# Operands of each stage prepared in the stage ahead of it, in a one-core transformer block on Trainium2

## Chip, cores, metric

One core of a Trainium2 chip runs the whole program. The metric is the device time of one execution in microseconds, as the median of several runs. Engines are named as in the profile: PE is TensorE (PEld its weight loads), DVE is VectorE, ACT is ScalarE, POOL is GpSimd, SP is SyncE, which here only issues loads and stores.

## The reference

One layer on x of 1024 tokens x 1024 features, float32. Retention runs over 4 heads in chunks of 128 tokens.

```python
h = rmsnorm(x, ln_mix)
z = h @ w_in                       # q | k | v | g | pu | gate_logits
ret_n = group_norm(retention_chunkwise(rotary(q), rotary(k), v)) * gn_gain
y_ret  = (silu(g) * ret_n) @ w_ret_up
y_pool = multiscale_pool(pu, pool_w, pool_scale) @ w_pool_up
gates  = sigmoid(gate_logits + b_gate)
x = x + (gates[..., :D] * y_ret + gates[..., D:] * y_pool) @ w_o
h2 = rmsnorm(x, ln_mlp)
x = x + square(relu(h2 @ w_up)) @ w_down        # w_up 1024 x 4096, w_down 4096 x 1024
return rmsnorm(x, ln_final)
```

## The kernel before

Features lie on the 128 partitions, tokens along the row, and most tiles are 128 x 512: one block of features by one half of the tokens. Every operand of a matmul is kept as a pair of a rounded high part and the remainder: `split_pair` (L131 to L133) has ACT write the copy (L132) and DVE the difference (L133); `split_weights` (L88 to L93) does so for 128 x 1024 weights. A product takes three matmuls for each contraction tile (`PASSES`): high by high, high by remainder, remainder by high.

The stages follow one another: q, k, v and retention; the swish gates (`ps_g`), with the pooling and `mixed_blocks` (block sums `hx` of the input for the gates) in the same loop over f; the branch gates, `gates(i)` for i < 8; the pool projection (`ps_yp`); the retention projection (`ps_yr`); the output projection (`ps_o`), which also makes the row sums of squares; up, `up(j)` for j < 16; down, in four sweeps over the same 16 j; the final norm.

Branch gates and up use `seven` (L178 to L219), which computes a 2 x 2 block product with seven block products instead of eight. It loads the weights `raw`, makes four sums of their blocks on DVE (`sum`, L204 to L215), splits each operand right ahead of its product, and collects in four PSUM banks `ps_X`, `ps_Y`, `ps_Z`, `ps_V`; each product is 12 matmuls (L191). `done` takes a finished bank over: for up a squared relu, scaled by the row's root R, and block sums of it (`act`), which POOL's queue stores to DRAM. The rest `u_up`, `tmp_up` are differences of finished banks.

Down uses the same seven products, written out by hand (L793 to L875), with `step` (L781) as one product into four banks, over four sweeps: X and Y, X and Z, V and Z, V. For each j it loads rows of `w_down` (`wa_`, `wb_`, `wc_`, `wd_`) and the stored blocks (`ad`), makes the weight sums (`sa`, `sb`, `sc`) and splits all (`da`, `db`, `ds`, `dt`), just ahead of that j's matmuls. After the second and third sweep the banks are added to the residual `x1b`, reloaded from DRAM, and ACT squares it (`add_squares`, L634 to L638). The last four j of the fourth sweep are taken for one output tile after the other (L875 to L887).

`token_rstd` makes the reciprocal root mean square of the tokens: PE transposes the sums (L160, four 128 x 128), DVE reduces them over 512 columns (L164) and scales (L142), POOL takes the power -1/2 (L145), PE spreads the result over the partitions (L151). `finish` (L732 to L747) multiplies by the gain on ACT (L738) and by the root on DVE or POOL (L743) and stores (L744).

A scheduler sets the order on each engine, when the program is built, from its own model of the times; on the chip every engine, and SP's queue of loads, then works through its list in order, and a row that waits holds up the rows behind it. Tiles come from pools with a fixed number of buffers (`h` and `r` 16 each, weights 4, `raw` 2, PSUM 5 banks and 3 more), so a load can start when the buffer's old tile has been read.

Of the kernel before, what the change touches and what calls it, by code (L numbers as in the profile page):

```python
# [38 lines left out]
def block_kernel(ctx: ExitStack, tc: tile.TileContext, a: dict, out: bass.AP):  # L39
# [19 lines left out]
    make_identity(nc, ident)  # L59
    nhalf = consts.tile([P, 4], F32, name="nhalf")  # L60
# [80 lines left out]
    def rstd_of(ssq, name, n):  # L141
        nc.vector.tensor_scalar(ssq, ssq, 1.0 / D, EPS, ALU.mult, ALU.add)  # L142
        tag = f"rstd_{name}" if name[0] == "a" else "rstd"
        rstd = stat.tile([P, n], F32, tag=tag, name=f"rstd_{name}")
        nc.gpsimd.tensor_tensor(rstd, ssq, nhalf[:, :n], ALU.pow)  # L145
        return rstd
# [9 lines left out]
    def token_rstd(sums, name):  # L156
        n = sums.shape[1] // P
# [6 lines left out]
        nc.vector.tensor_reduce(  # L164
            ssq, ps[:, : n * P].rearrange("p (t k) -> p t k", k=P),
            mybir.AxisListType.X, ALU.add,
        )
        return spread(rstd_of(ssq, name, n), n, name)
# [9 lines left out]
    def seven(name, src, moving, done):  # L178
# [5 lines left out]
        s1, s2, s3, s4 = (sums[:, i, :] for i in range(4))  # L184

        def mult(ps, src, x, start=True):
            w = pair_tile("a", f"w{x}_{name}")
            split_pair(w, src)
            for k in range(4):
                for n, (sa, sb) in enumerate(PASSES):  # L190
                    nc.tensor.matmul(  # L191
                        ps, w[:, sa, k * P : (k + 1) * P], moving[x][k][:, sb, :],
# [9 lines left out]
        mult(X, a11, B11)  # L202
        nc.scalar.activation(p1, X, AF.Copy)
        nc.vector.tensor_tensor(s1, a21, a22, ALU.add)  # L204
        nc.vector.tensor_tensor(s2, s1, a11, ALU.add)
        mult(Y, s2, T2)
        nc.vector.tensor_tensor(u2, p1, Y, ALU.subtract)
        mult(X, a12, B21, start=False)
        done(0, 0, X)
        mult(Z, s1, T1)  # L210
        nc.vector.tensor_tensor(u4, u2, Z, ALU.add)
        nc.vector.tensor_tensor(s3, a11, a21, ALU.add)
        mult(V, s3, T3)
        done(1, 1, V, u4)
        nc.vector.tensor_tensor(s4, a12, s2, ALU.add)  # L215
        mult(Z, s4, B22, start=False)
        done(0, 1, Z, u2)
        mult(V, a22, T4, start=False)
# [316 lines left out]
    for f in range(KT):  # L535
# [5 lines left out]
        if f in (2, 4, 5, 6):  # L541
            mixed_blocks((2, 4, 5, 6).index(f))
# [4 lines left out]
    def gates(i):  # L547
# [21 lines left out]
        seven(f"sg{i}", a["w_gate"][i], hx, done)  # L569
# [5 lines left out]
    ypT = []  # L575
    for f in range(4):
        y = a_tile("a", f"ypf{f}")
        nc.sync.dma_start(y, yp_dram[f])
        ypT.append([])
        for half in range(2):  # L580
            dst = pair_tile("h", f"ypT{f}_{half}")
            split_pair(dst, y[:, half * HALF : (half + 1) * HALF])
            ypT[f].append(dst)
# [103 lines left out]
    for half in range(2):  # L687
        sl = slice(half * HALF, (half + 1) * HALF)
        nc.vector.tensor_copy(R2[:, sl], token_rstd(sums2[:, half, :], f"b{half}"))


    def up(j):
# [24 lines left out]
        seven(f"up{j}", a["w_up"][j], h2, done)  # L717

    for j in range(NJ):
        up(j)  # L720


    outT = out.rearrange("(f p) t -> f p t", p=P)
    x1 = [None] * KT
# [7 lines left out]
    def finish(t0, n, R3, sizes):  # L732
        f0 = 0
        for size in sizes:
            o = a_tile("r", f"o_{t0}_{f0}", shape=(P, size, n))
            for i in range(size):
                f = f0 + i
                nc.scalar.activation(  # L738
                    o[:, i, :], x1[f][:, t0 : t0 + n], AF.Copy,
                    scale=vec[:, V_LNF + f : V_LNF + f + 1],  # L740
                )
# [77 lines left out]
    for i in UNITS:  # L819
        load_x1(i)  # L820
# [161 lines left out]
```

## Time and profile before

| | |
|---|---|
| Median of 3 runs | 1407.29 us (1406.32 to 1408.37) |
| Profiled execution | 1409.86 us |
| Its span, first to last instruction | 1408.1 us |
| Mean granted clock of PE | 0.988 |
| PE, DVE, ACT, POOL busy | 97%, 69%, 39%, 6% |
| Chain that ended last | PE 91%, DVE 4%, issue 2% |

Busy time is the time in which an instruction of the engine runs, matmuls at half clock included. The granted clock is TensorE's clock as a share of the full one. A wait is put down to the instruction that released it.

### The profile page before, as it was taken

The page shows a single profiled execution, that of the slowest core. Times are in us where ns is not written, and L with a number is a line of the kernel's source. Part 1 is how long each engine was busy: PE and PEld are TensorE (multiplying, and loading weights), DVE is VectorE, ACT ScalarE, POOL GpSimd, SP SyncE. Part 2 cuts the span into 40 slices and gives each one's busy share as a digit, 9 for nine tenths or more (in the row PEclk, how much of TensorE's full clock was granted, in tenths as well). Part 3 has the DMA queues.
Part 4 walks back from the last instruction along what each step waited for, and adds up shares of the span by engine and source line. Part 5 has one row for each costly group of instructions (what it writes and reads, how often), then busy time and mean ns, then how long its engine had stood idle before and what let it go on. Part 6 is the DMA issues. An engine that isn't in the chain of part 4 may idle for free.

```text
span 1408.1 us, 17330 instructions
## 1 busy us (share of the span) xinstructions
PE 1369.3 (97%) x6560; PEld 1147.6 (81%) x6560; DVE 969.9 (69%) x1605; ACT 545.5 (39%) x912; POOL 83.4 (6%) x139
## 2 busy tenths in 40 slices
PE   9999999999899999999999999999998999999985
PEld 6998999888688887888887788888887888878874
DVE  5766667767867645654558777877777867669583
ACT  6232424332534333321435333333333544335272
POOL 0000000100000000000000111111010000000001
PEclk9999999999999999999999999999999999999998
DMA  9111011232522328533322344343469977739251
GB/s 352 47 60 58 33 31 31 98 120 75 179 104 95 117 105 310 183 124 131 105 90 90 113 164 165 139 160 132 146 243 393 390 249 244 259 129 366 89 179 60
DMA packets 63572, 216.68 MB, mean 154 GB/s; under 512 B 7232, under 2 KB 9280, under 8 KB 59904
## 3 DMA queue, kind: packets, MB, share of 16 engines
q1 hardware_dynamic: 47648, 158.66, 32.2%
q0 software_dynamic: 15696, 56.89, 10.6%
q8 instruction: 51, 0.84, 0.3%
q14 instruction: 33, 0.27, 0.1%
q10 hardware_dynamic: 144, 0.03, 0.0%
HBM read 163.12 MB, written 52.43 MB: 153 GB/s over the span
## 4 chain that ended last, share of the span: by engine, by line
PE 91%; DVE 4%; issue 2%; DMA 1%; ACT 1%; POOL 0%; POOLq 0%; DVEq 0%; SPq 0%; ACTq 0%
PE ps_v L119 7%; PE ps_o L119 6%; PE ps_yr L119 6%; PE ps_dnX L781 6%; PE ps_Zup L191 6%; PE ps_Vup L191 6%; PE ps_Xup L191 6%; PE ps_dnV L781 6%; PE ps_dnZ L781 5%; PE ps_g L119 4%; PE ps_qT L119 3%; PE ps_Yup L191 3%; PE ps_pu L119 3%; PE ps_kT L119 3%; PE ps_dnY L781 3%; PE ps_Xsg L191 3%
## 5 line engine op out<-in xcount | busy, mean ns | idle before, releaser
L781 PE MATMUL ps_dnX<-db,da 128*128 128x512 f32 x384 | 94.1, 394 | 4.3 <-ACT db L132 4.3
L119 PE MATMUL ps_v<-w_v_hi,hT 128*128 128x256 f32 x512 | 95.9, 284 | 0.0
L191 PE MATMUL ps_Xup<-mv,w_up 128*128 128x512 f32 x384 | 94.3, 390 | 1.7 <-DVE w_up L133 1.5
L191 PE MATMUL ps_Zup<-mv,w_up 128*128 128x512 f32 x384 | 93.1, 390 | 0.3 <-ACT w_up L132 0.3
L191 PE MATMUL ps_Vup<-mv,w_up 128*128 128x512 f32 x384 | 93.0, 389 | 0.0
L119 PE MATMUL ps_g<-hT,w_g 128*128 128x512 f32 x384 | 90.6, 391 | 0.0
L781 PEld LDWEIGHTS ps_dnX<-db,da 128*128 128x128 f32 x384 | 73.1, 191 | 20.1 <-ACT db L132 4.7
L119 PE MATMUL ps_o<-mixT,w_o 128*128 128x512 f32 x384 | 87.5, 389 | 0.0
L119 PE MATMUL ps_yr<-retT,w_ret 128*128 128x512 f32 x384 | 87.2, 389 | 0.0
L191 PEld LDWEIGHTS ps_Xup<-mv,w_up 128*128 128x128 f32 x384 | 71.8, 188 | 17.3 <-DVE w_up L133 2.0
L191 PEld LDWEIGHTS ps_Zup<-mv,w_up 128*128 128x128 f32 x384 | 71.9, 188 | 15.9 <-ACT w_up L132 1.1
L119 PEld LDWEIGHTS ps_yr<-retT,w_ret 128*128 128x128 f32 x384 | 72.1, 188 | 15.0
L191 PEld LDWEIGHTS ps_Vup<-mv,w_up 128*128 128x128 f32 x384 | 72.1, 188 | 14.9
L119 PEld LDWEIGHTS ps_o<-mixT,w_o 128*128 128x128 f32 x384 | 72.0, 188 | 14.9
L119 PEld LDWEIGHTS ps_g<-hT,w_g 128*128 128x128 f32 x384 | 71.4, 188 | 14.4
L119 PEld LDWEIGHTS ps_v<-w_v_hi,hT 128*128 128x128 f32 x512 | 80.8, 192 | 0.0
L119 PE MATMUL ps_v<-w_v_lo,hT 128*128 128x256 f32 x256 | 72.7, 284 | 0.0
L699 ACT ACTIVATE act<-act 128x512 f32<-128x512 f32 x64 | 40.4, 632 | 76.9 <-DVE act L698 76.5
L132 ACT ACTIVATE w_up<-sum_up 128x512 fp32r<-128x512 f32 x64 | 39.8, 629 | 60.6 <-PE ps_Zup L191 23.6
L119 PE MATMUL ps_qT<-hT,w_qT 128*128 128x512 f32 x192 | 49.9, 407 | 1.8 <-ACT hT L136 1.5
L781 PE MATMUL ps_dnV<-dt,da 128*128 128x512 f32 (+1 forms) x204 | 46.3, 388 | 4.9 <-ACT dt L132 4.4
L132 ACT ACTIVATE w_up<-raw_up 128x512 fp32r<-128x512 f32 x48 | 30.1, 630 | 52.5 <-PE ps_Zup L191 25.5
(254 smaller groups left out, 2825.8 us busy)
## 6 DMA issues: line engine op xcount, KB each, us to landing
act_dram<-act POOLq DMA_DIRECT2D x48, 512.0 KB, 3.3
ad<-act_dram SPq DMA_DIRECT2D x48, 512.0 KB, 5.8
raw_up<-in_w_up_dram SPq DMA_DIRECT2D x16, 1024.0 KB, 5.0
raw_sg<-in_w_gate_dram SPq DMA_DIRECT2D x8, 1024.0 KB, 4.9
sg_dram<-sg POOLq DMA_DIRECT2D x16, 512.0 KB, 2.9
wa_lo<-in_w_down_dram SPq DMA_DIRECT2D x16, 512.0 KB, 9.0
wb_hi<-in_w_down_dram SPq DMA_DIRECT2D x16, 512.0 KB, 4.2
wc_lo<-in_w_down_dram SPq DMA_DIRECT2D x16, 512.0 KB, 5.2
```

The lines of the kernel that those rows point to most:

```text
L119: nc.tensor.matmul(ps, stationary(k, sa), moving(k, sb), start=i == 0, stop=i == n - 1)
L132: nc.scalar.activation(dst[:, 0, :], src, AF.Copy)
L191: nc.tensor.matmul(ps, w[:, sa, k * P : (k + 1) * P], moving[x][k][:, sb, :], start=start and k == 0 and n == 0, stop=k == 3 and n == 2, s ...
L699: nc.scalar.activation(dst, dst, AF.Square)
L781: nc.tensor.matmul(banks[i][:, c0 : c0 + n], w[:, sa, i * P : (i + 1) * P], x[:, sb, c0 : c0 + n], start=start and j == 0 and m == 0, stop ...
```

## The change

Six things change.

1. `token_rstd`: instead of the transposes and the reduce, matmuls with a column of ones write the sums of each 128 tokens into one PSUM column, which DVE scales straight from PSUM; with two parts, both are accumulated.
2. `seven` can take the last contraction tile of its first four products last (`late`, for gates(0) and up(0)), and has a hook `after`, called once X is done.
3. `mixed_blocks` runs at f = 1 to 4 instead of 2, 4, 5, 6.
4. The pooled operands are loaded and split in the last gate unit (`load_pooled`), the first two steps of down in the last unit of up (`begin_down`).
5. Down's operands are made from one list over all sweeps, three steps ahead (`prepare`); residual additions and squares are spread over the sweeps' steps.
6. At the end, the gains are applied ahead, DVE alone multiplies by the root, two tiles to an instruction and straight from PSUM, and the square of the last tile goes into the row sums as a second matmul.

```diff
@@ token_rstd @@
-            nc.tensor.transpose(
-                ps[:, t * P : (t + 1) * P], sums[:, t * P : (t + 1) * P], ident
-            )
-        ssq = stat.tile([P, n], F32, tag="ssq", name=f"ssq_{name}")
-        nc.vector.tensor_reduce(
...
+            for i, part in enumerate(sums):
+                nc.tensor.matmul(
+                    ps[:, t : t + 1], part[:, t * P : (t + 1) * P], ones[:, :1],
+                    start=i == 0, stop=i == len(sums) - 1,
+                )
+        return spread(rstd_of(ps[:, :n], name, n), n, name)
@@ seven @@
+        groups = {
+            B11: (X, (a11,)),
+            T2: (Y, (s2, (s1, a21, a22), (s2, s1, a11))),
+            T1: (Z, (s1,)),
+            T3: (V, (s3, (s3, a11, a21))),
+        }
+        rest = range(4)
+        if late:
+            rest = (3,)
+            for x, (ps, made) in groups.items():
+                stationary(x, *made)
+                mult(ps, x, range(3))
...
         done(0, 0, X)
-        mult(Z, s1, T1)
+        if after:
+            after()
+        opening(T1)
@@ swish loop @@
-        if f in (2, 4, 5, 6):
-            mixed_blocks((2, 4, 5, 6).index(f))
+        if 1 <= f <= 4:
+            mixed_blocks(f - 1)
@@ gates, up @@
+            f"sg{i}", a["w_gate"][i], hx, done, late=i == 0,
+            after=load_pooled if i == KT - 1 else None,
...
+            f"up{j}", a["w_up"][j], h2, done, late=j == 0,
+            after=begin_down if j == NJ - 1 else None,
@@ down @@
+    plan = [(ops, j) for ops in (operands_a, operands_b, operands_c, operands_d) for j in range(NJ)]
+    ready = []
+
+    def prepare(n):
+        while len(ready) < min(n, len(plan)):
+            ops, j = plan[len(ready)]
+            ready.append(ops(j))
+
+    def begin_down():
+        prepare(2)
...
+    def run(n, j, first, second=None, start=(True, True)):
+        prepare(n + 3)
+        for banks, wx, st in zip((first, second), ready[n], start):
+            step(banks, wx, j, start=st)
...
+    def residual(j):
+        if j % 2 == 0 and j < 8:
+            load_x1(j // 2)
+        if j % 2 == 1 and 2 < j < 11:
+            i = j // 2 - 1
+            add(x1[i][:, TH], x1[i][:, TH], u2[i])
...
+    def second_residual(j):
+        if j < 4:
+            add_squares(sums_all[:, T0], x1[j][:, T0], j == 0, f"z0_{j}", spare)
@@ end @@
+    def finish(i, t0, n, R3):
+        o = gained[t0 >= HALF, i][:, :, t0 % HALF : t0 % HALF + n]
+        nc.vector.tensor_tensor(
+            o, o, R3.rearrange("p (o t) -> p o t", o=1).to_broadcast([P, 2, n]), ALU.mult
+        )
...
+    for c0 in (0, 256):
+        c = slice(c0, c0 + 256)
+        last(3, c0, 256)
+        sq = spare(f"sq_z0_7_{c0}")[:, :256]
+        nc.scalar.activation(sq, x1[7][:, c], AF.Square)
...
+        ps = token_rstd([sums_all[:, c], sq], f"z0_{c0}")
+        pieces.append((c0, ps))
+    for c0, ps in pieces:
+        for i in UNITS:
+            finish(i, c0, 256, ps)
```

Where the instructions go. On PE at the change from up to down, before (`ps_Vup` collects the last of the seven products of up(15), with its weights `w_up`; `ps_dnX` are down's first banks):

```order
2326 L191 MATMUL ps_Zup_8270<-mv_3_6052,w_up_8359 128x512 x3
2327 L191 MATMUL ps_Vup_8271<-mv_0_5574,w_up_8382 128x512 x3
2328 L191 MATMUL ps_Vup_8271<-mv_1_5737,w_up_8382 128x512 x3
2329 L191 MATMUL ps_Vup_8271<-mv_2_5900,w_up_8382 128x512 x3
2330 L191 MATMUL ps_Vup_8271<-mv_3_6063,w_up_8382 128x512 x3
2331 L781 MATMUL ps_dnX_8403<-db_0_8422,da_0_8419 128x512
2332 L781 MATMUL ps_dnX_8404<-db_0_8422,da_0_8419 128x512
2333 L781 MATMUL ps_dnX_8405<-db_0_8422,da_0_8419 128x512
2334 L781 MATMUL ps_dnX_8406<-db_0_8422,da_0_8419 128x512
```

and now:

```order
2319 L195 MATMUL ps_Vup_8269<-mv_1_5725,w_up_8379 128x512 x3
2320 L195 MATMUL ps_Vup_8269<-mv_2_5888,w_up_8379 128x512 x3
2321 L195 MATMUL ps_Vup_8269<-mv_3_6051,w_up_8379 128x512 x3
2322 L854 MATMUL ps_dnX_8443<-db_0_8331,da_0_8328 128x512
2323 L854 MATMUL ps_dnX_8444<-db_0_8331,da_0_8328 128x512
2324 L854 MATMUL ps_dnX_8445<-db_0_8331,da_0_8328 128x512
2325 L854 MATMUL ps_dnX_8443<-db_0_8331,da_0_8328 128x512 x2
2326 L854 MATMUL ps_dnX_8444<-db_0_8331,da_0_8328 128x512 x2
2327 L854 MATMUL ps_dnX_8445<-db_0_8331,da_0_8328 128x512 x2
```

The first step of down now follows the fifth of the seven products; behind two steps into three banks each come the last two products of up(15), `ps_Zup` and `ps_Vup`, and then the fourth banks of those steps.

On ACT at the same place, before (`act_15` are the squares of the last unit of up, `da` to `dt` the copies for down):

```order
615 L699 ACTIVATE act_14_8116<-act_14_8116 128x512
616 L699 ACTIVATE act_15_8259<-act_15_8259 128x512
617 L699 ACTIVATE act_15_8261<-act_15_8261 128x512 x2
618 L699 ACTIVATE act_15_8260<-act_15_8260 128x512
619 L132 ACTIVATE da_0_8419<-wa_lo_8411 128x512
620 L132 ACTIVATE db_0_8422<-ad_0_8416 128x512
621 L132 ACTIVATE ds_0_8439<-sa_8418 128x512
```

and now:

```order
614 L730 ACTIVATE act_15_8257<-act_15_8257 128x512
615 L134 ACTIVATE da_0_8328<-wa_lo_8321 128x512
616 L134 ACTIVATE db_0_8331<-ad_0_8326 128x512
617 L134 ACTIVATE ds_0_8337<-sa_8334 128x512
618 L134 ACTIVATE dt_0_8340<-ad_0_8326 128x512
619 L134 ACTIVATE da_1_8347<-wa_lo_8343 128x512
620 L134 ACTIVATE db_1_8350<-ad_1_8345 128x512
621 L134 ACTIVATE ds_1_8356<-sa_8353 128x512
622 L134 ACTIVATE dt_1_8359<-ad_1_8345 128x512
623 L730 ACTIVATE act_15_8259<-act_15_8259 128x512 x2
624 L730 ACTIVATE act_15_8258<-act_15_8258 128x512
625 L134 ACTIVATE da_2_8458<-wa_lo_8451 128x512
```

The eight copies for the first two steps stand ahead of the last three squares; those of the third step are behind them.

On ACT at the change from the third to the fourth sweep, before (`sums_` and `sq_z` are squares of the residual, `o` its multiplication by the gain):

```order
820 L637 ACTIVATE sq_z_5_10614<-x1b_9840 128x512
821 L637 ACTIVATE sq_z_6_10619<-x1b_9843 128x512
822 L637 ACTIVATE sq_z_7_10624<-x1b_9846 128x512
823 L637 ACTIVATE sq_z_0_10629<-x1b_9837 128x512
824 L738 ACTIVATE o_0_10751<-x1b_9837,vec 128x512
825 L637 ACTIVATE sq_z_1_10634<-x1b_9840 128x512
826 L738 ACTIVATE o_1_10755<-x1b_9840,vec 128x512
827 L637 ACTIVATE sq_z_2_10639<-x1b_9843 128x512
828 L738 ACTIVATE o_2_10759<-x1b_9843,vec 128x512
829 L637 ACTIVATE sq_z_3_10644<-x1b_9846 128x512
830 L132 ACTIVATE da_0_10657<-wd_hi_10651 128x512
831 L132 ACTIVATE dt_0_10660<-ad_0_10652 128x512
```

and now:

```order
816 L134 ACTIVATE db_15_10543<-ad_15_10528 128x512
817 L134 ACTIVATE da_0_10576<-wd_hi_10570 128x512
818 L134 ACTIVATE dt_0_10579<-ad_0_10573 128x512
819 L134 ACTIVATE da_1_10606<-wd_hi_10570 128x512
820 L134 ACTIVATE dt_1_10609<-ad_0_10573 128x512
821 L665 ACTIVATE sums_8442<-x1b_9224 128x512
822 L931 ACTIVATE o_0_10690<-x1b_9224,vec 128x512
823 L668 ACTIVATE sq_z_1_10645<-x1b_9314 128x512
824 L931 ACTIVATE o_0_10690<-x1b_9314,vec 128x512
```

The first two pairs of copies stand ahead of the squares and the gains; the next pair follows eight squares and two gains.

## Rows read from the trace of the kernel before

**Rows 1.** The page, part 1: busy us, share of span, instructions by engine.
```profile
PE 1369.3 (97%) x6560; PEld 1147.6 (81%) x6560; DVE 969.9 (69%) x1605; ACT 545.5 (39%) x912; POOL 83.4 (6%) x139
```

**Rows 2.** Waits of PE: waited for, us in total, times, longest us.
```profile
PE spread_z L151 <- POOL rstd_z L145: 6.3, 2, 4.7
PE ps_dnV L781 <- ACT dt L132: 4.4, 1, 4.4
PE ps_dnX L781 <- ACT db L132: 4.3, 1, 4.3
PE ps_Ysg L191 <- ACT w_sg L132: 3.4, 1, 3.4
PE spread_b L151 <- POOL rstd_b L145: 2.0, 1, 2.0
...
PE ps_Xup L191 <- DVE w_up L133: 1.5, 1, 1.5
...
PE ps_yp L119 <- ACT w_po L92: 1.2, 1, 1.2
PE ps_Ysg L191 <- DVE w_sg L133: 1.2, 1, 1.2
```

**Rows 3.** Windows: span, PE, PEld, DVE, ACT, POOL busy (count), PEclk, DMA share, GB/s.
```profile
360.00:390.00 30.00, 25.38 (x101) 19.97 (x99) 25.16 (x41) 12.61 (x21) 1.60 (x3) 0.89 0.48 160
530.00:550.00 20.00, 18.42 (x81) 14.57 (x80) 14.27 (x21) 8.89 (x13) 1.59 (x3) 1.00 0.80 297
750.00:790.00 40.00, 36.08 (x156) 28.27 (x155) 33.89 (x57) 19.16 (x33) 5.37 (x4) 0.96 0.30 105
1060.00:1080.00 20.00, 15.71 (x63) 12.50 (x62) 14.56 (x24) 7.13 (x13) 2.13 (x4) 0.91 1.02 399
1100.00:1130.00 30.00, 30.00 (x134) 24.82 (x134) 24.66 (x41) 13.73 (x24) 0.00 (x0) 1.00 1.00 379
1240.00:1270.00 30.00, 28.70 (x125) 22.61 (x124) 24.69 (x41) 12.43 (x23) 0.00 (x0) 1.00 0.39 131
1330.00:1360.00 30.00, 25.58 (x110) 20.70 (x110) 24.03 (x40) 23.96 (x45) 1.31 (x1) 0.94 0.39 130
```

**Rows 4.** Timeline of PE, the end: start us, us, instruction, idle before.
```profile
1389.25 1.69 PE L781 MATMUL ps_dnV<-dt,da 128*128 128x256 f32 x12 [0.51 <-DVE x1b L880]
...
1400.59 0.69 PE L151 MATMUL spread_z<-ident,rstd_z 128*128 128x128 f32 x2 [4.66 <-POOL rstd_z L145]
```

**Rows 5.** Timeline of DVE, the end.
```profile
1396.37 3.21 DVE L743 TENSOR_TENSOR o<-o,R 128x256 f32<-128x256 f32 x4
1399.51 0.15 DVE L142 TENSOR_SCALAR ssq_z<-ssq_z 128x2 f32<-128x2 f32 x1
1401.31 2.73 DVE L743 TENSOR_TENSOR o<-o,spread_z 128x256 f32<-128x256 f32 x8 [1.64 <-PE spread_z L151]
```

**Rows 6.** Timeline of POOL, the end.
```profile
1395.99 3.31 POOL L743 TENSOR_TENSOR o<-o,R 128x256 f32<-128x256 f32 x4 [1.23 <-ACT R L885]
```

**Rows 7.** Timeline of PE, up to down.
```profile
1064.20 2.88 PE L191 MATMUL ps_Zup<-mv,w_up 128*128 128x512 f32 x12
...
1074.08 4.56 PE L781 MATMUL ps_dnX<-db,da 128*128 128x512 f32 x12 [4.29 <-ACT db L132]
```

**Rows 8.** Timeline of DVE, swish to branch gates.
```profile
373.30 0.68 DVE L205 TENSOR_TENSOR sum_sg<-sum_sg,raw_sg 128x512 f32<-128x512 f32 x1
```

**Rows 9.** Timeline of ACT, up to down.
```profile
1073.42 0.61 ACT L132 ACTIVATE db<-ad 128x512 fp32r<-128x512 f32 x1
```

**Rows 10.** Timeline of the tile ad, 1056 to 1058: the load of step 0.
```profile
L768 SPq DMA_DIRECT2D ad<-act_dram x1: 327/327/327, 1056.9 to 1056.9; - x1
...
DMA to landing us min/median/max: 8.1/8.1/8.1
```

**Rows 11.** Timeline of ACT, third to fourth sweep.
```profile
1341.99 0.61 ACT L637 ACTIVATE sq_z<-x1b 128x512 f32<-128x512 f32 x1
...
1343.03 0.61 ACT L132 ACTIVATE dt<-ad 128x512 fp32r<-128x512 f32 x1
```

More of the change, by code (lines that the diff above doesn't have):

```diff
@@ L176, in block_kernel, with seven @@
     B11, B21, B22, T1, T2, T3, T4 = range(7)
-    def seven(name, src, moving, done):
+    def seven(name, src, moving, done, late=False, after=None):
         raw = w_tile(f"raw_{name}", F32)
@@ L715, in done @@
                 nc.gpsimd.dma_start(act_dram[3][j], t4)
[L717 to L720 removed]
+        seven(
+            f"up{j}", a["w_up"][j], h2, done, late=j == 0,
+            after=begin_down if j == NJ - 1 else None,
+        )
     outT = out.rearrange("(f p) t -> f p t", p=P)
+    UNITS = range(4)
+    T0, TH = slice(0, HALF), slice(HALF, S)
     x1 = [None] * KT
@@ new lines, in block_kernel @@
+    Z = four("ps_dnZ", "aux")
+    def residual(j):
[4 more added lines that the diff above has]
+            add(x1[i][:, TH], x1[i][:, TH], u2[i])
+            y = x1[i + 4][:, T0]
+            nc.vector.tensor_tensor(y, y, u2[i], ALU.subtract)
+    sweep(1, X, Z, start=(False, True), then=residual)
+    for i in UNITS:
+        add(x1[i][:, T0], x1[i][:, T0], X[i])
+    V = four("ps_dnV")
+    for i in UNITS:
+        add(u4[i], u2[i], Z[i])
@@ new lines, in normalize, with last @@
+    def normalize(j):
+        if j < 4:
+            gain(2 * j, TH)
+            gain(2 * j + 1, TH)
+        if j == 3:
+            R3 = token_rstd([sums_all[:, TH]], "z1")
+            for i in UNITS:
+                finish(i, HALF, HALF, R3)
+        if 4 <= j < 8:
+            gain(j - 4, T0)
+    for j in range(NJ - NLAST):
+        run(3 * NJ + j, j, V, start=(False,))
+        normalize(j)
+    prepare(len(plan))
+    def last(i, c0, n):
+        for j in range(NJ - NLAST, NJ):
+            step(V, ready[3 * NJ + j][0], j, start=False, units=(i,), c0=c0, n=n)
+        y = x1[i + 4][:, c0 : c0 + n]
+        nc.vector.tensor_tensor(y, y, V[i][:, c0 : c0 + n], ALU.subtract)
@@ new lines, in block_kernel @@
+    for i in range(3):
+        last(i, 0, HALF)
+        add_squares(sums_all[:, T0], x1[i + 4][:, T0], False, f"z0_{i + 4}", spare)
+        gain(i + 4, T0)
+    pieces = []
+    for c0 in (0, 256):
[3 more added lines that the diff above has]
+        nc.scalar.activation(sq, x1[7][:, c], AF.Square)
+        nc.scalar.activation(
+            gained[False, 3][:, 1, c], x1[7][:, c], AF.Copy,
+            scale=vec[:, V_LNF + 7 : V_LNF + 8],
+        )
+        ps = token_rstd([sums_all[:, c], sq], f"z0_{c0}")
+        pieces.append((c0, ps))
```

258 lines of the change are left out of this document (121 added, 137 removed).

## Prediction

> **What bounds the kernel now.** The busy times come first [rows 1]: TensorE is busy for 1369.3 of 1408.1 us, so it sets the end and only its idle or half-speed time can be won. Next, what its idle time waited for [rows 2]: few waits, each long and met once. They stand where one stage hands over to the next. The windows [rows 3] price each handover. In mid-sweep (1100 to 1130) 134 matmuls start in 30 us, 0.224 us each. Length minus count times 0.224 is what a stage change loses, short transposes counted as full matmuls:
>
> - swish gates to branch gates, 360 to 390: 30 - 101 x 0.224 = 7.4
> - branch gates to pool projection, 530 to 550: 20 - 81 x 0.224 = 1.9
> - output projection to up, 750 to 790: 40 - 156 x 0.224 = 5.1
> - up to down, 1060 to 1080: 20 - 63 x 0.224 = 5.9
> - second to third sweep of down, 1240 to 1270: 30 - 125 x 0.224 = 2.0
> - third to fourth sweep, 1330 to 1360: 30 - 110 x 0.224 = 5.4
>
> Together 27.7 us; behind the last large matmul (ends about 1390.9) comes a serial tail of some 17 us [rows 4 to 6]. Part of the 27.7 is the clock: after the 4.3 us gap twelve matmuls take 4.56 us [rows 7] where twelve need 2.7, so 1.8 us; that is the lower of the two clock levels (1.2 and 2.4 GHz), granted clock 0.91 over the window. The short gap at 530 to 550 left the clock at 1.00 [rows 3].
>
> **The change part by part.** The matmuls of the stages stay; only their order and their operands' times move. Durations are of the profiled execution (1409.86 us; span 1408.1); the median of the three runs is 2.6 us lower, and the sum is taken off the median too.
>
> *Swish to branch gates: -6.5.* The second product waited 3.4 us for ScalarE's copy and 1.2 us for the remainder [rows 2], because the sum behind it ran only at 373.30 [rows 8], in VectorE's queue behind the block work of `mixed_blocks`, whose last part comes at f = 6 of 0 to 7. The change does that work at f = 1 to 4, so the weight load gets its buffer some 20 us earlier (my estimate: two f's of the loop, each 48 matmuls or 10.8). Counting the new VectorE row by row at 0.6 us each (the step between such rows), the copy is ready when TensorE arrives and the remainder up to 0.9 us late. Loss 7.4 to 0.9. Ends: 7.4, if nothing waits; 3, if the load comes late and the half clock stays. I take the value the count gives.
>
> *Branch gates to pool projection: +0.8.* `load_pooled` puts 8 copies on ScalarE and 8 remainders on VectorE inside the last gate unit. They stand ahead of the evacuation that frees the buffer of the next weight load, whose copy TensorE waited 1.2 us for [rows 2]. It comes later by up to four remainders at 0.6. Ends: 1.5 won, if the pooled operands were what delayed everything; 2 lost. I take 0.8 lost.
>
> *Output projection to up: -2.5.* The waits are 2.0 us for the root on POOL and 1.5 us for up's weights [rows 2], and the slower clock after (0.96). The row sums become one-column matmuls that VectorE reads at once, so its 512-wide reduce leaves the path, and three products whose last tile waits let TensorE run on meanwhile. The weights' remainder still stands behind the same copy. Ends 1 and 4.
>
> *Up to down: -2.5.* The first down operand waited for ScalarE's copy at 1073.42 [rows 9], behind the last activation's square. The change queues that copy ahead of the squares. TensorE now meets it 24 matmuls earlier: at 1064.20, where the last but one product starts [rows 7]. The load of `ad` was issued at 1056.9 and landed 8.1 us later [rows 10], at 1065.0; with 0.6 for the copy [rows 9], 1.4 us of waiting. The last two products then run, and step j = 2 needs copies behind the last square on ScalarE and five rows of the activation on VectorE: 12 matmuls (2.7) cover it but for 1.5, and the remainders for 0.4 more. Loss 5.9 to 3.3, rounded to 2.5 won. What is late next is therefore the landing, then j = 2. Ends 0 and 4.5.
> Gaps of 3.4 us and longer brought the lower clock, one of 1.2 did not [rows 2, 3]; mine are 1.4 and 1.5, so I charge no half clock. [...]
>
> *First to second sweep: 0.* No loss there and the same order now.
>
> *Second to third sweep: -1.6.* VectorE was full from 1250 on. Its four `x1b` additions, two of four sums and four further additions stood among the operands. Now the operands of j = 0 to 2 lie ahead of these, 21 rows at 0.6, and the additions share three steps that have 3 x 1.2 us of slack (a step is 24 matmuls, 5.4 us, against seven rows, 4.2). Loss 2.0 to 0.4.
>
> *Third to fourth sweep: -5.0.* TensorE waited 4.4 us for `dt` [rows 2]; ScalarE made it at 1343.03, after eight squares and three gains [rows 11]. Now the first two pairs are split ahead of any square. They cover 24 matmuls, 5.4 us; the copy of the third then comes 5.6 us after the sweep's start (eight squares and two gains at 0.52 to 0.6, and itself). Loss 5.4 to 0.4. Ends 3.5 and 5.4.
>
> *End: -3.6.* From the last matmul: sums (0.4), scaling and root and spread. The stretch from scaling at 1399.51 to spread at 1400.59 takes 1.1 [rows 4, 5], the spread 0.7. First products at 1393.3. Eight products read PSUM at 2.73 / 8 = 0.34 each [rows 5]; a pair of 256 is 512 wide, so 0.6 to 0.68. Four take 2.45; then, since VectorE has the second scaling queued behind them as before, 1.85; four more end at 1400.1, where the old ended at 1404.04. The last store is twice as large: 0.3 back. The four old products beside POOL's took 3.21 [rows 5, 6], 0.80 each: that price goes with POOL's part. Should broadcasting cost that much too, eight 512-wide products take 12.8 instead of 5, and the tail is 4 us longer than before. Ends 5 won, 1 won without that case.
>
> Sum: -6.5 + 0.8 - 2.5 - 2.5 - 1.6 - 5.0 - 3.6 = -20.9. Profiled execution 1389.0; median 1407.3 - 20.9 = **1386.4 us**.
>
> **The rivals.**
> 1. *Transfers arrive no earlier.* Over 1060 to 1080 the DMA share is 1.02 at 399 GB/s, full [rows 3]; the order on SP leaves eight 512 KB loads of `x1b` ahead of down's first operands. If earlier splits only wait for the same landings, up to down and output to up give nothing and the pool projection loses 2: -6.5 - 1.6 - 5.0 - 3.6 + 2 = -14.7, 1392.6 us. The 8.1 us landing speaks for it, the copy that waited 8 us beyond the landing against it.
> By the Trainium skill, "DMA: Bandwidth & Descriptors", section "Issuing engines are not separate DMA queues", transfers of any issuer share the same 16 engines and interleave; then an early request only slows those before it, which is this rival. Its figure of about 358 GB/s for the memory side is passed here by the window's 399.
> 2. *Short gaps bring the half clock.* Three remaining gaps at 1.8 us each: -15.5, 1391.8 us. The clock of 1.00 after the gap at 540 speaks against.
> 3. *All handovers close.* 27.7 + 3.6: 1376 us. Against it, the copies still behind the last activation.
> 4. *Slower: operands ahead of evacuations.* VectorE works in order, and twelve preparing rows now stand before the evacuation without which the last two products of up cannot run; likewise eight at the pool projection and the splits at the fourth sweep. If a row among them waits for a load issued only then, TensorE stands still for 8.1 us and 1.8 at half clock [rows 7, 10], some 10 us at each of the three: +30 against -20.9, about 1416 us. It decides from 7 us a place on. Against it: loads at the third place start in idle DMA (0.39 [rows 3]), and buffers come free as before.
> 5. *No effect*, gains and new waits cancelling: 1407.
>
> **How the numbers follow.** The forecast has a chance of 0.52 (its own range, 1380 to 1391), rival 1 0.20, rival 2 0.08, rival 3 0.08, rival 4 0.07, rival 5 0.05. A measurement of this kernel can tell about 0.2%, 2.8 us, from no change. Faster: 0.52 + 0.20 + 0.08 + 0.08 = 0.88; same 0.05; slower 0.07. The range leaves out rivals 3, 4 and 5, 0.20 in all, and takes in rivals 1 and 2 with their term bounds: 1379 to 1397 us.
>
> **What would show it.** TensorE's waits for `w_sg` and `dt` under 1 us; one of 1 to 2 us for `db` near 1050 to 1065 and one for `da` or `db` two steps later; the pool projection's wait for `w_po` at 2 to 3 us; granted clock near 1.00 at 370 and 1340; no POOL product in the tail, which is under 14 us. The prediction is wrong if a wait of over 3 us remains at a stage change, or if one appears inside a sweep.

## The result, and the profile after

The changed kernel takes 1388.86 us (median of 4 executions, 1388.35 to 1389.35). The kernel before took 1406.80 beside it on the same chip (4 executions, 1404.44 to 1408.37). The ratio is 0.9874, 95% interval 0.9857 to 0.9891: faster by about 17.9 us, against 20.9 forecast; 1386.4 was forecast, and the time lies 2.5 us above it. The profiled execution after took 1388.35 us, its span 1386.2 (before 1409.86 and 1408.1).

Busy time by engine (page, part 1) answers to [rows 1]:

```profile
PE 1365.0 (98%) x6584; PEld 1146.2 (83%) x6584; DVE 967.1 (70%) x1590; ACT 542.8 (39%) x903; POOL 77.9 (6%) x136
```

Of the 21.9 us of span only 4.3 are busy time of PE (1369.3 to 1365.0); the rest is idle time. The waits of PE, beside [rows 2]:

```profile
PE spread_z L153 <- POOL rstd_z L147: 3.0, 2, 1.9
PE ps_yp L121 <- ACT w_po L94: 1.7, 1, 1.7
PE ps_dnX L854 <- ACT db L134: 1.6, 1, 1.6
PE ps_Ysg L195 <- ACT w_sg L134: 1.4, 1, 1.4
PE ps_Xup L195 <- DVE w_up L135: 1.3, 1, 1.3
...
PE ps_dnX L854 <- DVE db L135: 1.1, 2, 0.8
...
PE ps_dnV L854 <- ACT dt L134: 0.5, 1, 0.5
PE ps_Zsg L195 <- DVE w_sg L135: 0.5, 1, 0.5
...
PE ps_Ysg L195 <- DVE w_sg L135: 0.4, 1, 0.4
```

No wait above 2 us is left. The one for `spread_b` no longer stands in the list, and those for `dt`, `db` and `w_sg` have shrunk from 4.4, 4.3 and 3.4. The windows at the same handovers, moved by roughly what the kernel leads there, with a mid-sweep one (1090 to 1120) as in [rows 3], same columns:

```profile
355.00:385.00 30.00, 28.19 (x117) 22.49 (x116) 22.22 (x35) 9.06 (x17) 1.42 (x3) 0.94 0.39 141
527.00:547.00 20.00, 18.29 (x81) 14.81 (x80) 12.98 (x18) 5.22 (x6) 1.59 (x3) 1.00 0.86 311
743.00:783.00 40.00, 38.65 (x182) 31.74 (x181) 34.03 (x58) 22.20 (x38) 3.57 (x4) 1.00 0.30 106
1052.00:1072.00 20.00, 19.23 (x85) 15.62 (x84) 13.11 (x21) 6.40 (x11) 0.00 (x0) 1.00 1.03 410
1090.00:1120.00 30.00, 30.00 (x134) 24.86 (x133) 28.09 (x47) 15.72 (x29) 0.00 (x0) 1.00 1.03 404
1228.00:1258.00 30.00, 30.00 (x134) 24.86 (x133) 27.98 (x47) 14.16 (x25) 0.00 (x0) 1.00 0.69 232
1315.00:1345.00 30.00, 29.50 (x135) 23.93 (x134) 20.52 (x31) 19.78 (x36) 1.03 (x1) 1.00 0.30 100
```

The second to third sweep (1228) looks like mid-sweep now, the third to fourth (1315) nearly so, and the granted clock at up to down has gone from 0.91 to 1.00. Only swish to branch gates (355) still loses clock. Where the time came from is read best from the last matmul of each stage, before and after. The table gives its start in us, which the profile shows for each tile; the gain of a part is the change in the distance from the row above. A handover's waits fall into the row below it: the first product of the branch gates runs ahead of the last `ps_g` matmuls, so swish to branch gates is in the row of `ps_g`, output to up in that of `ps_Yup`.

| start of the last matmul of | before | after | gain of this part | forecast |
|---|---|---|---|---|
| v | 225.8 | 224.5 | 1.3 | 0 |
| pooling input `ps_pu` | 341.7 | 340.9 | -0.5 | 0 |
| swish gates `ps_g` | 386.6 | 382.2 | 3.6 | 6.5 |
| branch gates `ps_Vsg` | 536.2 | 532.6 | -0.8 | } -0.8 |
| pool projection `ps_yp` | 581.9 | 578.2 | 0.1 | } |
| output projection `ps_o` | 756.5 | 753.2 | -0.4 | 0 |
| up `ps_Yup` | 1055.8 | 1047.9 | 4.6 | 2.5 |
| first sweep `ps_dnY` | 1162.6 | 1152.0 | 2.7 | 2.5 |
| second sweep `ps_dnX` | 1246.9 | 1236.4 | -0.1 | 0 |
| third sweep `ps_dnZ` | 1338.9 | 1326.1 | 2.3 | 1.6 |
| fourth sweep `ps_dnV` | 1390.7 | 1373.1 | 4.8 | 5.0 |
| end of span | 1408.1 | 1386.2 | 4.3 | 3.6 |

The first line is not the change: the profiled execution of before had its first 20 us at a granted clock of 0.91, the one after at 1.00, and other runs of the same code show either (below).

Up to down, PE, beside [rows 7]:

```profile
1056.27 0.84 PE L854 MATMUL ps_dnX<-db,da 128*128 128x512 f32 x3
1057.88 1.66 PE L854 MATMUL ps_dnX<-db,da 128*128 128x512 f32 x6 [0.77 <-DVE db L135]
...
1075.38 1.19 PE L854 MATMUL ps_dnX<-db,da 128*128 128x512 f32 x4 [1.57 <-ACT db L134]
1076.88 2.11 PE L854 MATMUL ps_dnX<-db,da 128*128 128x512 f32 x8 [0.30 <-DVE db L135]
```

The gap of 4.29 us has become 0.77 ahead of the last two products of up, and 1.57 and 0.30 at step j = 2. The end on PE and DVE, beside [rows 4, 5]:

```profile
1371.72 1.69 PE L854 MATMUL ps_dnV<-dt,da 128*128 128x256 f32 x12 [0.51 <-DVE x1b L965]
...
1375.30 0.61 PE L153 MATMUL spread_z<-ident,rstd_z 128*128 128x128 f32 x2 [1.10 <-POOL rstd_z L147]
...
1379.33 0.69 PE L153 MATMUL spread_z<-ident,rstd_z 128*128 128x128 f32 x2 [1.92 <-POOL rstd_z L147]
```

```profile
1374.31 0.16 DVE L146 TENSOR_SCALAR rstd_z<-sums_z 128x2 f32<-128x2 f32 x1 [0.44 <-PE sums_z L163]
1375.95 2.48 DVE L938 TENSOR_TENSOR o<-o,spread_z 128x512 f32<-128x512 f32 x4 [1.48 <-PE spread_z L153]
1378.35 0.15 DVE L146 TENSOR_SCALAR rstd_z<-sums_z 128x2 f32<-128x2 f32 x1
1380.06 2.48 DVE L938 TENSOR_TENSOR o<-o,spread_z 128x512 f32<-128x512 f32 x4 [1.55 <-PE spread_z L153]
```

The product over 512 columns with the root broadcast from PSUM takes 2.48 / 4 = 0.62 us, as estimated, and nothing stands on POOL beside it. From the start of the last large matmul, 1373.1, to the end of the span are 13.1 us; before it was 1408.1 - 1390.7 = 17.4.

### The profile page after: what moved, and what is told of

The parts are those of the page before. It is cut to its first block, busy times and chain, and to the rows that moved or that the text cites. A ratio compares the mean times of both kernels' runs of the same rounds, so it can differ in the third digit from the quotient of the medians.

```text
span 1386.2 us, 17348 instructions
## 1 busy us (share of the span) xinstructions
PE 1365.0 (98%) x6584; PEld 1146.2 (83%) x6584; DVE 967.1 (70%) x1590; ACT 542.8 (39%) x903; POOL 77.9 (6%) x136
## 4 chain that ended last, share of the span: by engine, by line
PE 91%; issue 5%; DVE 2%; DMA 1%; ACT 1%; POOL 0%; POOLq 0%; DVEq 0%; SPq 0%; ACTq 0%
PE ps_v L121 7%; PE ps_o L121 6%; PE ps_yr L121 6%; PE ps_Xup L195 6%; PE ps_Zup L195 6%; PE ps_dnX L854 6%; PE ps_dnZ L854 6%; PE ps_Vup L195 6%; PE ps_dnV L854 6%; PE ps_qT L121 3%; PE ps_g L121 3%; PE ps_yp L121 3%; PE ps_kT L121 3%; PE ps_Yup L195 3%; PE ps_Xsg L195 3%
## 5 line engine op out<-in xcount | busy, mean ns | idle before, releaser
L121 PEld LDWEIGHTS ps_v<-w_v_lo,hT 128*128 128x128 f32 x256 | 49.1, 192 | 0.0
```

What stands on the lines that cost most here:

```text
L121: nc.tensor.matmul(ps, stationary(k, sa), moving(k, sb), start=i == 0, stop=i == n - 1)
```

## The experiments

Each kernel is the changed one with the edit shown, so that undoing a part tells what that part carries. Below, a gain or loss at a handover is a difference of the distances in the table above, against the changed kernel's profile; it holds for the one execution that was profiled.

**Row sums by transposes again.**

```diff
-            for i, part in enumerate(sums):
-                nc.tensor.matmul(
-                    ps[:, t : t + 1], part[:, t * P : (t + 1) * P], ones[:, :1],
...
+            nc.tensor.transpose(
+                ps[:, t * P : (t + 1) * P], sums[0][:, t * P : (t + 1) * P], ident
+            )
+        ssq = stat.tile([P, n], F32, tag="ssq", name=f"ssq_{name}")
+        nc.vector.tensor_reduce(
...
```

(and at the end the last square is added on VectorE again)

> The changed kernel with the row sums made as before: transposes, a 512-wide reduce on VectorE, in the tail also the last square added on VectorE. From the anchors of the two profiles the change output projection to up gave 4.6 us and the end 4.3, both more than forecast. Theory: the reduce on VectorE's path made the 2.0 us wait for the root and the half clock behind it; with it back the wait for the spread returns to 1.5 to 2 us, the granted clock of the stage falls below 1, some 3 us are lost there and 1 at the end: about 1393. Rival: the products whose last tile waits carried that stage, the reduce was hidden; then only the end loses, about 1390.

Measured: 1391.80 us (1391.02 to 1394.59), ratio to before 0.9891 (0.9876 to 0.9905). Output to up is 4.4 us worse, of the 4.6 that the change had won there, and PE waits again, in the waits of this kernel:

```profile
PE spread_b L153 <- POOL rstd_b L147: 2.9, 1, 2.9
```

The end is 0.9 us longer, where 1 was expected. The late tile of the first unit is still in this kernel and covers nothing of that wait.

The reduce alone, 0.68 us on VectorE, does not make up the 2.9 us. From the end of PE's row sums of the second half to the end of POOL's power are 6.9 us here and 3.1 in the changed kernel. Of the difference 1.3 us lie ahead of POOL's row, in VectorE's queue, and 2.4 are that row itself, here and in the changed kernel:

```profile
770.42 3.81 POOL L147 TENSOR_TENSOR rstd_b<-rstd_b,nhalf 128x4 f32<-128x4 f32 x1 [13.97 <-DVE rstd_b L146]
```

```profile
768.21 1.41 POOL L147 TENSOR_TENSOR rstd_b<-rstd_b,nhalf 128x4 f32<-128x4 f32 x1 [12.98 <-DVE rstd_b L146]
```

For the first half it takes 1.03 in both, and before the change the second one took 3.21. Here VectorE runs its rows without a gap from 770.24 to 773.33, and POOL's ends 0.9 us after them; that they hold it up is likely, but was not tried alone.

**The late tile off.**

```diff
-            f"up{j}", a["w_up"][j], h2, done, late=j == 0,
+            f"up{j}", a["w_up"][j], h2, done, late=False,
```

(and the same for the gates)

> Only change from the changed kernel: the last contraction tile of the first unit's products is taken in its place again, in the gates and in up. Theory (the earlier runs put the 4.6 us won at output to up down to the row sums alone): the late tile is worth nothing there; what it would cover, the wait of the third product for up's weights (1.3 us), is there anyhow; same time as the changed kernel, 1387 to 1391 us. Rival: the late tile hides the root's way to the operands; then TensorE waits 1.5 to 3 us for the last tile of h2 at output to up, the lower clock may follow, and the time is 1390 to 1393 us.

Measured: 1388.96 us (1388.51 to 1391.62), 0.9870 (0.9853 to 0.9888), the time of the changed kernel. The profile is of the slowest of the four executions, 1391.62 us, and output to up is 2.0 us worse in it: the wait for `w_up` is 1.8 us instead of 1.3, and the ten matmuls behind it run at the lower clock, in this kernel and then in the changed one:

```profile
757.19 3.78 PE L195 MATMUL ps_Xup<-mv,w_up 128*128 128x512 f32 x10 [1.81 <-DVE w_up L135]
```

```profile
756.78 2.58 PE L195 MATMUL ps_Xup<-mv,w_up 128*128 128x512 f32 x10 [1.35 <-DVE w_up L135]
```

No wait for h2 appears. By the median the part is worth nothing; whether the longer wait and the lower clock in this one execution come from the edit stays open.

**The block work at its old places.**

```diff
-        if 1 <= f <= 4:
-            mixed_blocks(f - 1)
+        if f in (2, 4, 5, 6):
+            mixed_blocks((2, 4, 5, 6).index(f))
```

> The changed kernel with the block work of mixed_blocks at f = 2, 4, 5, 6 again. Swish to branch gates gave 3.6 us of the 6.5 forecast. Theory: those 3.6 come from the place of the block work alone; with it back the wait for w_sg is 3 us or more with half clock behind it, about 1392.5. Rival: they come from the products whose last tile waits and from the weight load's place; then the wait stays near 1.4 us and the time within 0.5 us of 1388.9.

Measured: 1391.88 us (1390.78 to 1393.51), 0.9888 (0.9874 to 0.9903). The handover is 2.5 us worse, most of its 3.6; what made the other 1.1 was not traced. The first of its waits is shorter than the 3.4 of [rows 2], the second the same:

```profile
373.29 1.22 PE L195 MATMUL ps_Ysg<-hx,w_sg 128*128 128x512 f32 x2 [2.29 <-ACT w_sg L134]
375.69 4.49 PE L195 MATMUL ps_Ysg<-hx,w_sg 128*128 128x512 f32 x10 [1.18 <-DVE w_sg L135]
```

**Down's first operands after up.**

```diff
-            after=begin_down if j == NJ - 1 else None,
```

> The changed kernel without the hook in the last unit of up, so that the first operands of down are split after its activations. Theory: the wait of over 4 us for db before the first down matmul returns, with the half clock behind it, 2.7 us in all: about 1391.6. Rival (transfers arrive no earlier): the wait was for the landing and the order of the splits is worth nothing, within 0.5 us of 1388.9.

Measured: 1390.77 us (1388.65 to 1392.84), 0.9880 (0.9862 to 0.9897). In the profile the single gap is back, 4.29 us instead of 0.77 + 1.57 + 0.30 = 2.64, with the lower clock after it; together 3.9 us:

```profile
1067.02 5.49 PE L853 MATMUL ps_dnX<-db,da 128*128 128x512 f32 x12 [4.29 <-ACT db L134]
```

But the four executions stand in two pairs, 1388.65 and 1388.86, 1392.68 and 1392.84, and the lower pair equals the changed kernel. So 1.65 us of idle time are shown in the trace; how much of them the median gains, these four don't settle.

**One step ahead instead of three.**

```diff
-        prepare(n + 3)
+        prepare(n + 1)
```

> The changed kernel with operands made one step ahead instead of three, the first two steps of down still early. Theory: the third to fourth sweep loses its 4.8 us again (first pair behind eight squares, a wait of about 4 us with half clock), the second to third its 2.3: about 1396. Rival: the spreading of the residual's additions over the sweeps carried the second to third sweep; then only the 4.8 return, about 1393.5.

Measured: 1397.69 us (1397.24 to 1400.00), 0.9934 (0.9918 to 0.9951). Third to fourth sweep is 8.0 us worse: PE waits 5.9 us for `dt`, and the granted clock in 1320 to 1350 is 0.89. Second to third sweep differs by 0.1 us.

```profile
1333.46 2.08 PE L854 MATMUL ps_dnV<-dt,da 128*128 128x512 f32 x4 [5.92 <-ACT dt L134]
```

That is 3.2 us more than before the change (55.0 against 51.8), so the edit does not bring back the old order there; it shows that without the look-ahead nothing of the 4.8 is left. Of the 2.3 at the second to third sweep the look-ahead carries nothing.

**Why `w_sg` still waits: another buffer for the pooling's output.** In the changed kernel ScalarE's timeline at swish to branch gates shows this:

```profile
357.18 0.63 ACT L134 ACTIVATE w_sg<-raw_sg 128x512 fp32r<-128x512 f32 x1 [1.64 <-DMA raw_sg<-in_w_gate_dram]
359.95 1.68 ACT L134 ACTIVATE hx<-xw 128x512 fp32r<-128x512 f32 x3 [2.14 <-DMA yp_dram<-yp]
...
365.73 1.67 ACT L134 ACTIVATE w_sg<-sum_sg 128x512 fp32r<-128x512 f32 x3 [2.60 <-DVE sum_sg L188]
```

The copies of the block operands `hx` wait for a store of `yp`, because both take their buffers from the pool `r`, and the weight sums stand behind them on VectorE. The edit gives `yp` a buffer of another pool:

```diff
-        y = a_tile("r", f"yp{f}")
+        y = a_tile("a", f"yp{f}")
```

> Only change from the changed kernel: the output tile of the pooling takes its buffer from the weight sums' pool of buffers rather than from the one that also holds the rounded operands. Theory: at swish to branch gates the splits of the block operands waited for such a buffer until the tile's store was done (ScalarE waited 2.1 us for that store), and that is why TensorE still waits 1.4 and 0.4 us for w_sg; with another buffer both waits go, and the half clock behind them: 1.5 to 3.3 us better at this handover, 1385 to 1387.5 us. Rival: the weights' load, issued only 14 us ahead of its first product, sets the time; the waits stay and the time is 1388 to 1391 us.

Measured: 1384.38 us (1383.60 to 1384.70), 0.9838 (0.9820 to 0.9855). The copy of the sum comes at 361.54 instead of 365.73, and the product runs through without a gap; the granted clock in 355 to 385 is 1.00:

```profile
365.76 2.88 PE L195 MATMUL ps_Ysg<-hx,w_sg 128*128 128x512 f32 x12
```

The handover is 4.1 us better, more than the 1.5 to 3.3 expected, and all four executions lie below those of the changed kernel. (The buffers of the weight sums lie in the pool of the weights, not in `a`, other than the expectation says.)

Of the 4.1, 1.7 are clock that the same code does not lose in every execution. Three other kernels of this section change nothing up to this place: pooled operands behind the last unit, one step ahead, two products on POOL. They keep the full clock there behind waits of 0.9 to 1.1 and 0.4 us; from the pooling input to the swish gates they take 39.2 to 39.4 us, the changed kernel 41.3, this one 37.2. Two more (row sums by transposes, three steps) lost it behind 1.1 and 0.4. The matmuls behind the second wait, in the changed kernel and with one step ahead:

```profile
367.55 3.87 PE L195 MATMUL ps_Ysg<-hx,w_sg 128*128 128x512 f32 x10 [0.41 <-DVE w_sg L135]
371.22 11.39 PE L121 MATMUL ps_g<-hT,w_g 128*128 128x512 f32 x48
```

```profile
368.65 2.56 PE L195 MATMUL ps_Ysg<-hx,w_sg 128*128 128x512 f32 x10 [0.40 <-DVE w_sg L135]
371.05 11.04 PE L121 MATMUL ps_g<-hT,w_g 128*128 128x512 f32 x48
```

**Both: old places, other buffer.** The two edits above in one kernel.

> The run with the block work at its old places (f = 2, 4, 5, 6) and the run with the pooling's output in another pool of buffers, both in one kernel; the rest as changed. Theory: the wait for the buffer's store is one cause, the place of the block work a second one, and they add: with the old places and the new buffer TensorE waits 1 to 3 us for w_sg, between the 3.7 us of the old places and the zero of the new buffer; handover 1.5 to 4.5 us worse than with the new buffer alone, time 1386 to 1389 us. Rival: the buffer alone was the cause, early or late block work only changes how long a store is waited for; then no wait for w_sg is left and the time is 1384 to 1385.5 us.

Measured: 1389.56 us (1388.83 to 1392.54), 0.9880 (0.9866 to 0.9893). The handover is as with the old places alone (2.6 us worse than the changed kernel, against 2.5), and PE waits:

```profile
PE ps_Ysg L195 <- ACT w_sg L134: 2.6, 1, 2.6
...
PE ps_Ysg L195 <- DVE w_sg L135: 0.6, 1, 0.6
```

Neither expectation holds as it stood: the causes don't add, they lie in a row. With the old places the first weight sum runs at 370.63, behind the last blocks in VectorE's queue, and in the kernel with the old places alone no row waits for the store of `yp`. (The median is 2.3 us below that of the old places alone, but the executions overlap, and at this handover the two profiles differ by 0.1.) Only when the blocks have moved forward does the buffer become the last wait.

**Pooled operands behind the last gate unit.**

```diff
-            after=load_pooled if i == KT - 1 else None,
...
+    load_pooled()
```

> Only change from the changed kernel: the pooled operands are loaded and split behind the last gate unit instead of inside it. Theory of the prediction (early splitting delays the evacuation and with it the next weights, 0.8 us lost): 0.5 to 1 us better at gates to pool projection, the waits for w_po (1.7 us) and for the gate unit's remainder (0.5 us) gone or down to 1.2 us together. Rival: the pooled operands then arrive late instead, and TensorE waits 1.5 to 3 us for them: 1.5 us or more lost there. Either way the total stays within 1386 to 1392 us, so the trace of this stage decides, not the total.

Measured: 1387.05 us (1385.28 to 1388.15), 0.9857 (0.9841 to 0.9872). The branch gates' part is 0.8 us better, with the wait for `w_sg` of 0.48 gone, and `w_po` waits 1.25 + 0.32 instead of 1.71. (Another 2.0 us come from swish to branch gates, where this profile shows the full clock and the edit does nothing.) But the split is not shown to be the cause: the other buffer, the old places and both together leave it inside the last unit, and their branch gates take 149.6 us too, against 150.4, without that wait. In them, as here, PE's products of the last unit stand in another order than in the changed kernel.

**Three steps ahead of up's last products.**

```diff
     def begin_down():
-        prepare(2)
+        prepare(3)
```

> Only change from the changed kernel: three steps of down's operands instead of two are prepared ahead of the last two products of up. Theory: the wait of 1.6 us for the copy of db and of 0.3 us for its remainder at step j = 2 comes from its rows standing behind the last activation; moved ahead of it, they are ready, and 1.9 us go, or up to 3.4 with the half clock that follows this gap in some executions: 1385.5 to 1387.5 us. Rival: the loads for j = 2 have not landed by then, and ScalarE and VectorE, which work in order, hold up the last activation: a wait of 1.5 to 4 us moves to the last two products of up or to dnY, 1389 to 1393 us.

Measured: 1388.33 us (1386.13 to 1389.62), 0.9865 (0.9850 to 0.9881). Step 2 now runs ahead of up's last two products, and its copy of `db` is waited for there, 0.93 us; another 0.28 follows at step 3. From up to the end of the first sweep the profile shows 0.0 us of difference. The wait moved, as the rival has it, though it is smaller; nothing is won.

**Two products of the end on POOL again.**

```diff
+        eng = nc.gpsimd if t0 == 0 and i < 2 else nc.vector
-        nc.vector.tensor_tensor(
+        eng.tensor_tensor(
```

(the first piece's root is copied to SBUF by ScalarE for it)

> Only change from the changed kernel: at the end, two of the four products of the first piece go to POOL again, which reads the root from a copy that ScalarE makes in SBUF. Theory of the prediction: a product of VectorE beside POOL's costs more than alone (0.80 against 0.34 us for 256 columns before; 0.62 for 512 columns alone now); then VectorE's two products beside POOL take 1.0 to 1.6 us each, and the end comes no earlier: 1388 to 1391 us. Rival: VectorE is not slowed (0.62 each); its second scaling then comes 1.2 us earlier and so does the end: 1386.5 to 1388 us.

Measured: 1388.64 us (1388.33 to 1390.74), 0.9872 (0.9859 to 0.9886); the end is 1.1 us longer in the profile. The products of the first piece, by engine (min/median/max in ns):

```profile
L939 DVE TENSOR_TENSOR o<-o,R_first x2: 691/1220/1750, 1375.4 to 1376.0; 128x512 f32<-128x512 f32 x2
L939 POOL TENSOR_TENSOR o<-o,R_first x2: 1699/1732/1766, 1375.4 to 1377.2; 128x512 f32<-128x512 f32 x2
```

VectorE's first product, which starts just ahead of POOL's, takes 0.69 us; its second, which starts while POOL's runs, takes 1.75 and ends 0.6 after POOL's first; together 2.36 us, where two alone take 1.24. POOL's second then runs to 1378.8, and the second root on POOL stands behind it.

**Three parts in one kernel.** The other buffer, the pooled operands behind the last unit, and at the end:

```diff
-        ps = token_rstd([sums_all[:, c], sq], f"z0_{c0}")
-        pieces.append((c0, ps))
+        pieces.append((c0, token_rstd([sums_all[:, c], sq], f"z0_{c0}", later=True)))
+    pieces = [(c0, spread(rstd, 2, f"z0_{c0}")) for c0, rstd in pieces]
```

(`later` returns the root without spreading it)

> Three changes to the changed kernel together: the pooling's output in another pool of buffers (4.5 us better by itself), the pooled operands split behind the last gate unit (1.8 us by the medians, 0.8 us by its trace), and at the end the row sums and roots of both pieces ahead of the first spread, so that the second scaling no longer stands behind four products in VectorE's queue. Theory: the parts lie at different handovers and add: 4.1 + 0.8 + 1.0 to 1.6 at the end, 1382.0 to 1383.5 us, and VectorE's eight last products run without the idle time of 1.55 us between the fourth and the fifth. Rival: the end is set by the stores, not by VectorE's products, or the second sums delay the first spread by as much: nothing won at the end, 1383.5 to 1385 us.

Measured, in 5 executions: 1383.52 us (1382.80 to 1384.14), 0.9834 (0.9821 to 0.9848): 5.3 us below the changed kernel and the best of all. The end is 1.1 us shorter, with the eight products in a row:

```profile
1371.65 4.87 DVE L939 TENSOR_TENSOR o<-o,spread_z 128x512 f32<-128x512 f32 x8 [0.24 <-PE spread_z L153]
```

Against the kernel with the other buffer alone the medians differ by 0.9 us, and the executions of the two overlap (1383.60 to 1384.70 there). The median lies on the border between the theory's range and the rival's; the profile shows the end won, as in the theory, and the pooled operands worth nothing on top of the buffer: branch gates and pool projection together take 195.3 us, with the buffer alone 195.2. The first sweep lost 1.7 us to the lower clock in this profile.

## Why the prediction was right, and where its terms were off

The forecast held: a gain of 20.9 us was summed, and the two profiled executions differ by 1409.86 - 1388.35 = 21.5 us, of which 1.3 are the clock of the first 20 us. That the sum came so close is in part luck: swish to branch gates gave 2.9 us less than its term, while output to up gave 2.1 more, and the second to third sweep and the end 0.7 more each.

The time alone does not decide against rival 2: it lies 2.5 us above the forecast and 2.9 below that rival's 1391.8. The traces decide better (last point below). Of rival 1, transfers arriving no earlier, PE's rows from 1056 on show the contrary (0.77 us of waiting, and that for VectorE), and rival 4 is not seen: no wait of over 2 us stands anywhere. Of the signs that were named, the wait for `dt` (0.5 us), the one two steps later (1.57), the clock at the fourth sweep (1.00) and the tail without a POOL product (13.1 us) came; the wait for `w_sg` (1.4, under 1 was named), the first one for `db` (0.77, not 1 to 2), the one for `w_po` (1.7, not 2 to 3) and the clock near 370 (0.94) did not.

- **The median against the profile.** The sum was made on an execution of 1409.86 and then taken off a median of 1407.29. The execution lay 2.6 us above that median, the one profiled after lies 0.5 below its own; so the medians gained less than the profiles did, 17.9 against 21.5 us, and the time came out 2.5 us above 1386.4 though the terms sum to nearly what the profiles show. Where the 2.6 come from was not traced. The lower clock at the start, 1.3 us, is nothing special to that execution: eight of the other twelve profiles show it too.
- **Swish to branch gates, -6.5, measured -3.6.** The term was mis-sized, and the step that failed is the count by which "the copy is ready when TensorE arrives and the remainder up to 0.9 us late". It put at nothing that the block copies could wait for a buffer; they waited 2.14 us for the store of `yp`, and TensorE waited 1.40 + 0.41 = 1.81 us for `w_sg`. It also charged no lower clock behind so short a wait, which cost another 1.7 us here (0.94). "The weight load gets its buffer some 20 us earlier" was wrong too: it was issued at 352.18, before at 360.10, so 7.9 us earlier. But that did not set the time: with the other buffer it is issued at 353.22, and nothing waits. With the other buffer the handover gives 3.6 + 4.1 = 7.7, more than was forecast.
- **Branch gates to pool projection, +0.8, measured +0.7.** Right in size, but not by the way that was foreseen. The copy of `w_po` was to come later; PE waits 1.71 us for it, against 1.19 + 0.40 before. The loss lies ahead of it, inside the branch gates, with a new wait of 0.48 us for `w_sg`. Undoing the early split won 0.8 us there, and so did three kernels that keep it, so its cause stays open.
- **Output to up, -2.5, measured -4.6.** The upper end was 4, and it lay beyond it. The row sums alone carry it (4.4 of 4.6 with them undone), and by more than the reduce that the prediction named: POOL's row for the root took 3.21 us before and 1.41 after. The late tile, to which the prediction gave a share, is worth nothing by the medians. What remains is the wait for `w_up`, 1.35, as said.
- **Up to down, -2.5, measured -2.7.** The first wait was 0.77 where 1.4 was forecast (the load was issued at 1047.22 and landed 7.3 us later, at 1054.5), the second 1.57 + 0.30 where 1.5 + 0.4 was.
- **Second to third sweep, -1.6, measured -2.3.** Right in size; of the cause, the three steps of look-ahead are excluded. That spreading the additions over the sweep is what does it is likely, but was not tried alone.
- **Third to fourth sweep, -5.0, measured -4.8.** The remaining gap is 0.49 where 0.4 was forecast, and without the look-ahead nothing of the gain is left.
- **End, -3.6, measured -4.3.** The broadcast cost nothing extra (0.62 a product), and the price of POOL beside VectorE was real. VectorE's last product ends 3.9 us earlier behind the last large matmul than before, as summed (9.4 against 13.3 us); the rest is the last store, for which 0.3 us was charged and which takes 3.7 us to the end of the span instead of 4.1.
- **Rival 2, that short gaps bring the half clock,** is true in part, and was given as an either-or where it is neither. In the changed kernel's profile the lower clock followed the gaps at swish to branch gates (0.94) and not those at up to down (1.00). After the same gap of 1.57 us at step j = 2, nine profiles (the changed kernel's and eight of the others) show the full clock seven times and the lower one twice. Two of them, the block work at its old places without and with the other buffer:

```profile
1077.90 1.20 PE L854 MATMUL ps_dnX<-db,da 128*128 128x512 f32 x4 [1.57 <-ACT db L134]
1079.39 3.61 PE L854 MATMUL ps_dnX<-db,da 128*128 128x512 f32 x8 [0.29 <-DVE db L135]
```

```profile
1077.68 1.20 PE L854 MATMUL ps_dnX<-db,da 128*128 128x512 f32 x4 [1.57 <-ACT db L134]
1079.17 2.11 PE L854 MATMUL ps_dnX<-db,da 128*128 128x512 f32 x8 [0.30 <-DVE db L135]
```

Eight matmuls take 3.61 us in one and 2.11 in the other, behind the same gaps; granted clock 0.93 and 1.00 in 1070 to 1095. It costs 1.5 us there and 1.7 to the end of the sweep. The argument that a gap of 1.2 us had not brought the lower clock, and so those of 1.4 and 1.5 would not, rested on one execution, and it left out a third case of its own rows: the wait of 2.0 us for `spread_b` [rows 2], in a window at 0.96 [rows 3]. The Trainium skill, "TensorE: Matmul & The Clock Gate", section "Why this matters for your kernels", warns of idle gaps between bursts that are longer than these. For the gap of 4.29 us before the change the trace agrees; here the lower clock also follows gaps below 2 us, in one execution and not in the next.

## What to carry to other kernels

Where a queue is worked in order, ask of an operand that comes late not only what stands ahead of it but which buffer it needs and whose store or read frees that buffer: here 2.5 us hung on moving the work forward, and another 4.1, 1.7 of them clock, on one letter, the buffer's pool. Causes that lie in a row don't add: the buffer alone, with the work at its old place, was worth nothing at that handover. A sum made on one profiled execution is to be compared with that execution, and the distance of that execution from the median said as an uncertainty of its own.

## What was not expected of the hardware

- The same idle gap is followed by either clock, by execution, as shown above. The start of the program does the same: 0 to 20 us ran at a granted clock of 1.00 in the changed kernel's profile and three others, at 0.91 in the rest, and before; at the last matmul of v the latest and the earliest of these profiles lie 1.8 us apart (226.1 and 224.3), though no edit touches that stretch.
- VectorE beside POOL is not slowed evenly: one product of two took 0.69 us and the other 1.75, ending 0.6 us after POOL's. The Trainium skill, "SBUF — State Buffer", section "SBUF: two separate sides", says that a VectorE operation with two SBUF inputs and a GpSimd operation that reads SBUF exclude each other for a whole instruction; the second product's time agrees with that, the first one's shows nothing against it.
- Row sums as matmuls into one column are not cheaper on PE than the transposes: in 744 to 775 eight of them take 0.95 us, four transposes 0.60 in the run with the old sums. What they win lies on the other engines: VectorE's reduce over 512 columns (0.68 us) falls away, and POOL's row for the second root takes 1.41 us instead of 3.81.
- In 1052 to 1072 the transfers moved 410 GB/s at a DMA share of 1.03 while TensorE lost only 0.77 us: the 512 KB load of `ad` took 7.3 us to land, but it had been asked for early enough to cover that.
